# A mixture of experts as a software pipeline: the second layer of a tile behind the first layer of the next, with the weights loaded in that order

## The chip, the core and the metric

The kernel runs on one core of one Trainium2 chip. The metric is the device time of one execution in microseconds; lower is better. The core has TensorE (PE, matmuls; PEld is its weight load), VectorE (DVE), ScalarE (ACT), GpSimd (POOL) and SyncE (SP, which here only issues loads and stores), and 16 DMA engines that all queues share.

## The reference, cut to what matters

One transformer-like layer: an adaptive norm, a time-mixing branch and a recurrent branch, their merge, and then a layer of experts, of which each token takes two out of 32. The change touches only the experts:

```python
for e in range(N_EXPERTS):                      # 32
    he = jax.nn.silu(t @ w1e[e]) * (t @ w3e[e]) # t: 1024 tokens x 1024; w1e, w3e: 1024 x 256
    out = out + cw[:, e:e + 1] * (he @ w2e[e])  # w2e: 256 x 1024; cw is 0 for experts not taken
```

All is in float32.

## The kernel before, in words

Everything before the experts (up to about 1131 us of 1528) and the final norm behind them are the same before and after.

**Lists.** After the router each expert has a list of its tokens. The experts other than 0, 1 and 2 are sorted by load, and the list of each gets a place with a fixed capacity (256, 224, 192, 128, 112, 96, 80, 64 or 32 rows). A *job* is one tile of up to 128 rows. There are 26 jobs: 20 tiles of *single* experts (16 experts; four of them have two tiles), 4 *pairs* (two experts of 64 rows side by side) and 2 *fours* (four experts of 32 rows). The order of the jobs is three singles, a pair, five tiles of singles, a four, a pair, seven tiles of singles, a pair, three tiles of singles, a four, two singles, a pair. What doesn't fit goes to overflow tiles behind all that, in a chain of conditions, of which none runs here.

**Weights.** Each expert is 6 *pieces* of 128 x 1024 float32, 512 KB each: pieces 0 to 3 are the first layer (w1 and w3), pieces 4 and 5 the second (w2). `issue` puts the loads on SP's queue in the order of the list `pieces`; a piece goes to one of `NRAW` = 16 raw buffers (`w`). For a single expert `split` turns a piece into a high part `wh` (cast on ACT to the fast matmul format) and a low part `wl` (raw minus high, on DVE, or on POOL for pieces 4 and 5, except for the first two experts); `NW` = 8 buffers of each. The raw buffer is free again after the split. Pairs and fours use the raw pieces directly, in full float32, and hold them until their matmuls have read them.

**One job.** `gather` fetches the token rows from HBM by an indirect DMA on POOL into one of two buffers `xg`. `turn` transposes them on TensorE (8 transposes) and splits them into `th` and `tl`. `up` is the first layer: 24 matmuls (8 slices of 128 rows, three products high-high, high-low, low-high). `hidden` does SiLU on ACT, the product on DVE (`he`) and two transposes. `down` splits that into `eh` and `el`, runs the second layer, 12 matmuls, multiplies by a row (`yt`, DVE) and scatters the rows by an indirect DMA on POOL. `turn2`, `up2`, `down2` are the same for pairs and fours, without splits, with matmuls on parts of the columns that run side by side.

**Order.** The Python text gives each instruction its priority; a scheduler of the framework puts each engine's instructions into a fixed order at build time, by that priority and by when it believes operands and buffers to be ready. At run time every engine goes through its queue in order. The text of the loop before is, for job n: gather of n+1, first layer of n, transposes of n+1, hidden step and second layer of n, `issue` up to 18 pieces past the job's own, splits of the next expert.

Of the kernel before, what the change touches and what calls it, by code (L numbers as in the profile page):

```python
# [9 lines left out]
F32 = mybir.dt.float32  # L10
# [7 lines left out]
DRAM = bass.MemoryType.DRAM  # L18

NRAW = 16  # L20
NW = 8
LA = 3
ONPOOL = (4, 5)
C0 = math.exp(-0.5)
# [68 lines left out]
def _build(tc, A, out, dump, stop, top):  # L93
# [857 lines left out]
              [tuple(NS + 2 * NP + 4 * i + q for q in range(4)) for i in range(NQ)]]  # L951

    jobs = [((e,), e, 128) for e in range(NF)]
    order, pieces, upto = [], [(e, c) for e in range(NF) for c in range(6)], {e: 6 * e + 6 for e in range(NF)}
    for _, u in sorted(((i + 0.5) / len(us), u) for us in units for i, u in enumerate(us)):
        es = tuple(NF + len(order) + q for q in range(len(u)))
        order += u
        pieces += [(e, c) for c in range(6) for e in es]
        for e in es:
            upto[e] = len(pieces)  # L960
        if len(u) == 1:
            jobs += [(es, t, m) for t, m in tiles_of(u[0])]
        elif len(u) == 2:
            jobs.append((es, NTP + (u[0] - NS) // 2, 128))
        else:
            jobs.append((es, NTQ + (u[0] - NS - 2 * NP) // 4, 128))
    raws, src = {}, {}
    issued = [0]

# [4 lines left out]
    def load(src, c, raw=None):  # L974
        raw = wo.tile([128, 1024], F32, name="w", bufs=NRAW) if raw is None else raw
        Y.dma_start(raw, src[:, c * 1024:c * 1024 + 1024])
        return raw

    def issue(n):

        while issued[0] < min(n, 192):
            e, c = pieces[issued[0]]
            if e not in src:
                src[e] = A["we"][e] if e < NF else chosen(order[e - NF])
            raws[e, c] = load(src[e], c)
            issued[0] += 1
# [332 lines left out]
    with pool("psume", 1, PSUM) as psum, pool("ew", 1) as ew, pool("ex", 2) as ex:  # L1319
# [1 line left out]
        for t in xgb:  # L1321
            P.memset(t, 0.0)

        def split(raw, pool_engine):
            h = ew.tile([128, 1024], F32R, name="wh", bufs=NW)
            l = ew.tile([128, 1024], F32R, name="wl", bufs=NW)
            S.copy(h, raw)  # L1327
            (P if pool_engine else V).tensor_sub(l, raw, h.bitcast(F32))  # L1328
            return h, l

        def gather(n, ti, m):

            xg = xgb[n % 2]
            P.indirect_dma_start(out=xg[0:m], out_offset=None, in_=h2d,
                                 in_offset=bass.IndirectOffsetOnAxis(ap=gidx[0:m, ti:ti + 1], axis=0),
                                 bounds_check=1023, oob_is_err=False)
            return xg

        def turn(xg, m):

            R = slice(0, m)
            th = ex.tile([128, 8, 128], F32R, name="th")
            tl = ex.tile([128, 8, 128], F32R, name="tl")
            for i in range(2):
                pt = psum.tile([128, 4, 128], F32, name="pt", bufs=3)
                for k in range(4):
                    T.transpose(pt[:, k, R], xg[R, (4 * i + k) * 128:(4 * i + k) * 128 + 128], ident[R, R])
                sl = slice(4 * i, 4 * i + 4)
                S.copy(th[:, sl, R], pt[:, :, R])  # L1349
                V.tensor_sub(tl[:, sl, R], pt[:, :, R], th[:, sl, R].bitcast(F32))  # L1350
            return th, tl
# [13 lines left out]
        def hidden(ph, m):  # L1365

            R = slice(0, m)
            he = ex.tile([128, 256], F32, name="he")
            S.activation(he[R], ph[R, 0:256], AF.Silu)
            V.tensor_mul(he[R], he[R], ph[R, 256:512])  # L1370
            pt = psum.tile([128, 4, 128], F32, name="pt", bufs=3)
            for k in range(2):
                T.transpose(pt[:, k, R], he[R, k * 128:k * 128 + 128], ident[R, R])
            return pt
# [3 lines left out]
            P.indirect_dma_start(out=yd, out_offset=bass.IndirectOffsetOnAxis(ap=sidx[R, ti:ti + 1], axis=0),  # L1378
                                 in_=yt[R], in_offset=None, bounds_check=2047, oob_is_err=False)

        def down(W, ph, ti, m):
            R = slice(0, m)
            pt = hidden(ph, m)
            eh = ex.tile([128, 2, 128], F32R, name="eh")
            el = ex.tile([128, 2, 128], F32R, name="el")
            S.copy(eh[:, :, R], pt[:, 0:2, R])
            V.tensor_sub(el[:, :, R], pt[:, 0:2, R], eh[:, :, R].bitcast(F32))
            yt = ex.tile([128, 1024], F32, name="yt")
            for hf in range(2):
                sl = slice(hf * 512, hf * 512 + 512)  # L1390
                py_ = psum.tile([128, 512], F32, name="py", bufs=3)
                for k in range(2):
                    h, l = W[4 + k]
                    o = hf * 512
                    T.matmul(py_[R], eh[:, k, R], h[:, o:o + 512], start=(k == 0), stop=False)
                    T.matmul(py_[R], eh[:, k, R], l[:, o:o + 512], start=False, stop=False)
                    T.matmul(py_[R], el[:, k, R], h[:, o:o + 512], start=False, stop=(k == 1))
                V.tensor_mul(yt[R, sl], py_[R], mrow["gt2"][R, sl])
            scatter(yt, ti, m)
# [3 lines left out]
        def turn2(xg):  # L1403
            tp = ex.tile([128, 8, 128], F32, name="th")
            for i in range(2):
                pt = psum.tile([128, 4, 128], F32, name="pt", bufs=3)
                for k in range(4):
                    T.transpose(pt[:, k], xg[:, (4 * i + k) * 128:(4 * i + k) * 128 + 128], ident)
                S.copy(tp[:, 4 * i:4 * i + 4], pt)
            return tp  # L1410
# [5 lines left out]
        def up2(W, tp):  # L1416
            ph = psum.tile([128, 512], F32, name="ph", bufs=2)
            for k in range(8):
                o = (k % 2) * 512
                for s_, C in parts(W):  # L1420
                    T.matmul(ph[C], tp[:, k, C], W[s_][k // 2][:, o:o + 512], start=(k == 0), stop=(k == 7))  # L1421
            return ph

        def down2(W, ph, ti):
            pt = hidden(ph, 128)
            ep = ex.tile([128, 2, 128], F32, name="eh")
            S.copy(ep, pt[:, 0:2])
            yt = ex.tile([128, 1024], F32, name="yt")
            for hf in range(2):
                sl = slice(hf * 512, hf * 512 + 512)  # L1430
                py_ = psum.tile([128, 512], F32, name="py", bufs=3)
                for k in range(2):
                    for s_, C in parts(W):
                        T.matmul(py_[C], ep[:, k, C], W[s_][4 + k][:, sl], start=(k == 0), stop=(k == 1))
                V.tensor_mul(yt[:, sl], py_, mrow["gt2"][:, sl])  # L1435
            scatter(yt, ti, 128)

        W = {}

        def begin(es):  # L1440
            for e in es:
                if e not in W:
                    W[e] = [raws.pop((e, c)) for c in range(6)]
                    if len(es) == 1:
                        if e < 2:
                            with tc.issue_after(last.ins):
                                W[e] = [split(r, False) for r in W[e]]
                        else:
                            W[e] = [split(r, c in ONPOOL) for c, r in enumerate(W[e])]

        def turned_of(n, xg):
            es, _, m = jobs[n]
            return turn2(xg) if len(es) > 1 else turn(xg, m)

        issue(6 * LA)
        begin(jobs[0][0])
        tt = {0: turned_of(0, gather(0, *jobs[0][1:]))}
        for n, (es, ti, m) in enumerate(jobs):
            nxt = jobs[n + 1] if n + 1 < len(jobs) else None
            if nxt:  # L1460
                xg = gather(n + 1, *nxt[1:])
            pair = len(es) > 1
            ph = up2([W[e] for e in es], tt.pop(n)) if pair else up(W[es[0]], tt.pop(n), m)
            if nxt:
                tt[n + 1] = turned_of(n + 1, xg)
            if pair:
                down2([W[e] for e in es], ph, ti)
            else:
                down(W[es[0]], ph, ti, m)
            if nxt and nxt[0] != es:  # L1470
                issue(max(upto[es[-1]] + 6 * LA, upto[nxt[0][-1]]))
                begin(nxt[0])


        shf, scf, gf = (wo.tile([128, 1024], F32, name="w", bufs=NRAW) for _ in range(3))
# [8 lines left out]
        def nest(o):  # L1484
            if o < NX:
                with tc.If(cnt > o):
                    we = chosen(32 + o)
                    w = [split(load(we, c, ex.tile([128, 1024], F32, name="yt")), c in ONPOOL) for c in range(6)]
                    tt_ = turn(gather(o, NT0 + o, 128), 128)
                    down(w, up(w, tt_, 128), NT0 + o, 128)  # L1490
                    nest(o + 1)
        nest(0)

# [37 lines left out]
```

## Time and profile before

| | |
|---|---|
| median of 3 runs | 1531.28 us (1524.67 to 1535.25) |
| the profiled execution's own time | 1529.99 us |
| its span | 1528.2 us |
| TensorE busy | 1321.9 us, 87% |
| DVE, ACT, POOL busy | 60%, 32%, 26% |
| weight loads of the experts | 192 of 512 KB |
| bytes moved in the whole span | 248.58 MB, mean 163 GB/s |

The span runs from the first to the last instruction; the execution's time is a little longer. Shares over the whole span mix stages with different limits, so the rows below are read by stretches, in us from the span's start. "Waited for" rows give the idle time of an engine and the instruction that ended it. Matmuls are pipelined, so the duration of one (about 0.4 us) is longer than the distance to the next.

### The profile page before, as it was taken

Reading aid. Unit: us, or ns where it says so; the run is one execution under the profiler, and the core shown is the slowest. Engines: PE = TensorE matmul, PEld = TensorE weight load, DVE = VectorE, ACT = ScalarE, POOL = GpSimd, SP = SyncE. Lnnn points to the kernel's source line nnn. Section 1 sums busy time; section 2 is a strip of 40 time slices with the busy share of each in tenths; the row PEclk is TensorE's granted clock in tenths of the full one; section 3 lists DMA queues with packets and bytes.
Section 4 is the critical chain, followed back from the end, with each engine's and each line's share of the span. In section 5 each row is a group of like instructions: output and inputs, shape, how many; then the busy total and the mean of one; then the engine's idle time right before and its main releaser. Section 6 shows DMA issues by size and latency. Waiting matters only on the chain.

```text
span 1528.2 us, 23082 instructions
## 1 busy us (share of the span) xinstructions
PE 1321.9 (87%) x8482; PEld 919.1 (60%) x8482; DVE 917.9 (60%) x2071; ACT 487.0 (32%) x892; POOL 402.5 (26%) x331
## 2 busy tenths in 40 slices
PE   0999899899999999999999798899848998989810
PEld 0776676666776667766666476687645644745400
DVE  8936868687758562475532587724686524653457
ACT  3222323132222222222221594312335423532421
POOL 7001222121101210111111325701214522743314
PEclk9998999899999999999999899999959999999965
DMA  6334432323442211112210654442358979978962
GB/s 263 128 120 138 124 113 90 101 94 115 140 151 87 73 59 36 45 47 69 64 49 27 210 191 147 156 159 95 113 192 299 382 275 401 379 275 313 410 275 101
DMA packets 112827, 248.58 MB, mean 163 GB/s; under 512 B 39056, under 2 KB 40384, under 8 KB 111680
## 3 DMA queue, kind: packets, MB, share of 16 engines
q1 hardware_dynamic: 105952, 230.22, 43.4%
q0 software_dynamic: 6752, 16.79, 3.0%
q8 instruction: 69, 1.13, 0.3%
q14 instruction: 54, 0.44, 0.1%
HBM read 217.11 MB, written 37.31 MB: 166 GB/s over the span
## 4 chain that ended last, share of the span: by engine, by line
PE 58%; DVE 19%; DMA 12%; ACT 4%; issue 4%; POOL 3%; SPq 0%; POOLq 0%; DVEq 0%; ACTq 0%
DMA w<-in_we 9%; PE pg L318 6%; PE pg L319 6%; PE pg L320 6%; PE pj L318 3%; PE pj L320 2%; PE pj L319 2%; PE st L603 2%; DVE wa L228 2%; PE st L617 2%; PE pj L1129 2%; PE pj L1128 2%; PE pj L1127 2%; PE ph L1421 2%; PE ph L1360 1%
## 5 line engine op out<-in xcount | busy, mean ns | idle before, releaser
L318 PE MATMUL pg<-hh,wh 128*128 128x512 f32 x376 | 160.2, 426 | 8.1 <-DVE cr L680 5.9
L319 PE MATMUL pg<-hl,wh 128*128 128x512 f32 x376 | 158.2, 421 | 0.0
L320 PE MATMUL pg<-hh,wl 128*128 128x512 f32 x376 | 156.9, 417 | 0.0
L560 POOL TENSOR_TENSOR WV<-VT,m 128x512 f32<-128x512 f32 x32 | 35.6, 1112 | 371.2 <-PE st L603 283.5
L1327 ACT CAST wh<-w 128x1024 fp32r<-128x1024 f32 x96 | 98.4, 1051 | 56.6 <-PE ph L1362 21.0
L1328 DVE TENSOR_TENSOR wl<-w,wh 128x1024 fp32r<-128x1024 f32 x68 | 89.9, 1346 | 17.3 <-ACT wh L1327 14.2
L228 DVE SCALAR_TENSOR_TENSOR wa<-wa,cb 128x1024 f32<-128x1024 f32 x64 | 80.0, 1257 | 28.7 <-DMA wa<-in_wada 28.7
L318 PEld LDWEIGHTS pg<-hh,wh 128*128 128x128 f32 x376 | 73.0, 194 | 33.3 <-issue 12.5
L216 ACT CAST wh<-wr 128x512 fp32r<-128x512 f32 x88 | 54.4, 618 | 100.2 <-PE pj L319 48.4
L217 DVE TENSOR_TENSOR wl<-wr,wh 128x512 fp32r<-128x512 f32 x72 | 55.1, 766 | 50.9 <-ACT wh L216 50.6
L319 PEld LDWEIGHTS pg<-hl,wh 128*128 128x128 f32 x376 | 72.8, 194 | 17.8 <-issue 4.7
L320 PEld LDWEIGHTS pg<-hh,wl 128*128 128x128 f32 x376 | 72.5, 193 | 17.6 <-issue 4.0
L610 DVE SCALAR_TENSOR_TENSOR St<-St,Dc,st 128x64 f32<-128x64 f32 x128 | 35.4, 277 | 77.8 <-PE st L608 77.7
L318 PE MATMUL pj<-hh,wh 128*128 128x512 f32 x192 | 77.5, 404 | 1.1 <-DVE carry L365 1.1
L320 PE MATMUL pj<-hh,wl 128*128 128x512 f32 x192 | 77.0, 401 | 0.0
L319 PE MATMUL pj<-hl,wh 128*128 128x512 f32 x192 | 75.7, 394 | 0.0
L1328 POOL TENSOR_TENSOR wl<-w,wh 128x1024 fp32r<-128x1024 f32 x28 | 68.6, 2455 | 19.0 <-ACT wh L1327 12.5
L1360 PE MATMUL ph<-wh,th 128*128 128x512 f32 (+4 forms) x160 | 64.8, 407 | 6.2 <-ACT th L1349 5.6
L515 DVE TENSOR_TENSOR X<-X,UC 128x60 f32<-128x60 f32 (+24 forms) x248 | 67.0, 270 | 4.2
L1378 POOL DMA_INDIRECT yd<-yt,sidx x26 | 41.7, 1606 | 99.8 <-DVE yt L1435 41.6
L1361 PE MATMUL ph<-wl,th 128*128 128x512 f32 (+4 forms) x160 | 64.2, 401 | 4.0 <-DVE wl L1328 3.9
L1362 PE MATMUL ph<-wh,tl 128*128 128x512 f32 (+4 forms) x160 | 63.7, 399 | 1.7 <-DVE tl L1350 1.7
(512 smaller groups left out, 3136.1 us busy)
## 6 DMA issues: line engine op xcount, KB each, us to landing
w<-in_we SPq DMA_DIRECT2D x192, 512.0 KB
wa<-in_wada SPq DMA_DIRECT2D x64, 512.0 KB
wr<-in_win SPq DMA_DIRECT2D x72, 256.0 KB
gd<-gt SPq DMA_DIRECT2D x32, 256.0 KB
g<-gd SPq DMA_DIRECT2D x32, 256.0 KB
yy<-yd SPq DMA_DIRECT2D x8, 1024.0 KB
xT<-in_xT SPq DMA_DIRECT2D x8, 512.0 KB
Ui<-Ud SPq DMA_DIRECT2D x32, 128.0 KB
```

Of the source, the lines that this page charges most:

```text
L216: S.copy(h[:, :n], raw)
L217: eng.tensor_sub(l[:, :n], raw, h[:, :n].bitcast(F32))
L228: V.scalar_tensor_tensor(wa, wa, 1.0, cb, op0=OP.mult, op1=OP.mult, accum_out=ccol[:, i:i + 1])
L318: T.matmul(ps, wh[:, o:o + 128], hh[k][:, sl], start=(k == 0), stop=False)
L319: T.matmul(ps, wh[:, o:o + 128], hl[k][:, sl], start=False, stop=False)
L320: T.matmul(ps, wl[:, o:o + 128], hh[k][:, sl], start=False, stop=(k == n - 1))
L515: V.tensor_add(X[:, :nj, s + 1:32], X[:, :nj, s + 1:32], t_)
L1327: S.copy(h, raw)
L1328: (P if pool_engine else V).tensor_sub(l, raw, h.bitcast(F32))
L1360: T.matmul(ph[R], th[:, k, R], h[:, o:o + 512], start=(k == 0), stop=False)
L1361: T.matmul(ph[R], th[:, k, R], l[:, o:o + 512], start=False, stop=False)
L1362: T.matmul(ph[R], tl[:, k, R], h[:, o:o + 512], start=False, stop=(k == 7))
```

## The change

The loop over jobs is written as a pipeline. In iteration n the text now has: gather of n+3, first layer of n+1 (with `issue` and the splits of its pieces 0 to 3 in front), the splits of pieces 4 and 5 of n, hidden step of n, transposes of n+2, second layer of n. The list `pieces` follows that: the first-layer pieces of a unit (a single expert, a pair or a four), then the second-layer pieces of the unit before. The 8 buffers for split pieces become two pools: 5 for first-layer pieces (`whu`, `wlu`) and 3 for second-layer pieces (`whd`, `wld`).

```diff
-NW = 8
+NWU, NWD = 5, 3
...
+    pieces, upto = [], {}
+    for i in range(len(units_) + 1):
+        pieces += [(e, c) for c in range(4) for e in units_[i]] if i < len(units_) else []
+        pieces += [(e, c) for c in (4, 5) for e in units_[i - 1]] if i else []
+        if i:
+            upto[units_[i - 1]] = len(pieces)
...
-        def split(raw, pool_engine):
-            h = ew.tile([128, 1024], F32R, name="wh", bufs=NW)
-            l = ew.tile([128, 1024], F32R, name="wl", bufs=NW)
+        def split(raw, c, pool_engine):
+            n, b = ("u", NWU) if c < 4 else ("d", NWD)
+            h = ew.tile([128, 1024], F32R, name="wh" + n, bufs=b)
+            l = ew.tile([128, 1024], F32R, name="wl" + n, bufs=b)
...
+        def first(n):
+
+            if n < len(jobs):
+                es, _, m = jobs[n]
+                issue(upto[es] + 6 * (LA - 2))
+                begin(es, range(4))
+                ph[n] = up2(weights(es), tt.pop(n)) if len(es) > 1 else up(weights(es), tt.pop(n), m)
...
         issue(6 * LA)
-        begin(jobs[0][0])
-        tt = {0: turned_of(0, gather(0, *jobs[0][1:]))}
+        fetch(0)
+        turned_of(0)
+        fetch(1)
+        fetch(2)
+        first(0)
+        turned_of(1)
         for n, (es, ti, m) in enumerate(jobs):
-            nxt = jobs[n + 1] if n + 1 < len(jobs) else None
-            if nxt:
-                xg = gather(n + 1, *nxt[1:])
+            fetch(n + 3)
+            first(n + 1)
+            begin(es, (4, 5))
             pair = len(es) > 1
-            ph = up2([W[e] for e in es], tt.pop(n)) if pair else up(W[es[0]], tt.pop(n), m)
-            if nxt:
-                tt[n + 1] = turned_of(n + 1, xg)
+            pt = hidden(ph.pop(n), 128 if pair else m)
+            turned_of(n + 2)
             if pair:
-                down2([W[e] for e in es], ph, ti)
+                down2(weights(es), pt, ti)
             else:
-                down(W[es[0]], ph, ti, m)
-            if nxt and nxt[0] != es:
-                issue(max(upto[es[-1]] + 6 * LA, upto[nxt[0][-1]]))
-                begin(nxt[0])
+                down(weights(es), pt, ti, m)
```

`fetch(n)` is the gather of job n, `turned_of(n)` its transposes, `begin(es, cs)` takes the raw pieces `cs` of the experts and splits them where the expert is a single one, `weights(es)` hands the pieces to the matmuls. No instruction of the computation is added or removed.

## Rows read from the trace of the kernel before

**Rows 1.** Stretches: PE, PEld, DVE, ACT, POOL busy (count), clock, DMA share, GB/s.
```profile
1131.00:1180.00 49.00, 39.96 (x176) 29.31 (x177) 33.67 (x42) 25.54 (x33) 22.25 (x13) 0.88 0.87 291
1180.00:1216.00 36.00, 34.44 (x163) 22.30 (x160) 19.46 (x27) 17.75 (x27) 18.75 (x11) 1.00 1.02 387
1216.00:1250.00 34.00, 33.12 (x190) 17.92 (x188) 10.52 (x19) 9.65 (x19) 11.63 (x9) 1.00 0.73 247
1250.00:1336.00 86.00, 76.38 (x325) 45.68 (x324) 44.13 (x54) 35.96 (x50) 38.25 (x21) 1.00 1.02 393
1336.00:1366.00 30.00, 26.77 (x119) 15.64 (x118) 15.85 (x18) 13.07 (x19) 16.24 (x9) 0.94 0.69 245
1366.00:1390.00 24.00, 20.84 (x102) 12.62 (x100) 12.17 (x16) 9.08 (x17) 8.20 (x6) 1.00 1.02 394
1390.00:1408.00 18.00, 17.89 (x100) 9.29 (x104) 4.57 (x9) 2.14 (x7) 6.88 (x6) 1.00 0.61 207
1408.00:1450.00 42.00, 37.13 (x176) 18.91 (x170) 18.75 (x23) 17.44 (x24) 14.84 (x8) 1.00 1.02 409
```
**Rows 2.** Waits of SP's queue, expert stage: total us, times, longest.
```profile
SPq L976 <- DVE wl L1328: 54.0, 37, 10.9
SPq L976 <- POOL wl L1328: 40.7, 18, 3.1
```
**Rows 3.** Timeline of TensorE: start, duration, line (first and 21st of a run).
```profile
1210.02 0.39 PE L1360 MATMUL ph<-wh,th 128*128 128x512 f32 x1
...
1214.56 0.39 PE L1362 MATMUL ph<-wh,tl 128*128 128x512 f32 x1
```
**Rows 4.** Waits of TensorE, 1148 to 1236.
```profile
PE ph L1360 <- ACT th L1349: 3.1, 6, 1.1
PE pt L1373 <- DVE he L1370: 2.9, 4, 2.0
```
**Rows 5.** Waits of TensorE, 1291 to 1354.
```profile
PE pt L1373 <- DVE he L1370: 3.9, 3, 3.2
PE ph L1360 <- ACT th L1349: 1.3, 3, 0.6
```
**Rows 6.** Waits of TensorE, 1354 to 1400.
```profile
PE ph L1362 <- DVE tl L1350: 1.7, 1, 1.7
PE ph L1360 <- ACT th L1349: 1.2, 3, 0.5
```
**Rows 7.** The chain that ended last, one piece of it.
```profile
1165.20 5.09 DMA w<-in_we
```
**Rows 8.** Timeline of DVE and TensorE around 1339 (idle time in brackets).
```profile
1334.62 7.62 DVE L1328 TENSOR_TENSOR wl<-w,wh 128x1024 fp32r<-128x1024 f32 x4
...
1342.63 0.41 PE L1373 MATMUL pt<-ident,he 112*128 112x112 f32 x2 [3.18 <-DVE he L1370]
```
**Rows 9.** Groups by line, 1100 to 1530: busy us, mean ns, idle before.
```profile
L1327 ACT CAST wh<-w 128x1024 fp32r<-128x1024 f32 x95 | 97.4, 1052 | 56.6 <-PE ph L1362 21.0 <-DMA w<-in_we 14.3 <-issue 10.7
L1328 DVE TENSOR_TENSOR wl<-w,wh 128x1024 fp32r<-128x1024 f32 x68 | 89.9, 1346 | 17.3 <-ACT wh L1327 14.2 <-DMA w<-in_we 2.6
L1328 POOL TENSOR_TENSOR wl<-w,wh 128x1024 fp32r<-128x1024 f32 x28 | 68.6, 2455 | 19.0 <-ACT wh L1327 12.5 <-issue 6.2
...
L1378 POOL DMA_INDIRECT yd<-yt,sidx x26 | 41.7, 1606 | 99.8 <-DVE yt L1435 41.6 <-DVE yt L1398 32.9 <-DMA w<-in_we 11.7
...
L1334 POOL DMA_INDIRECT xg<-h2d,gidx x26 | 28.4, 1092 | 93.2 <-PE pt L1347 50.7 <-PE pt L1408 22.1 <-DVE ef L1309 18.5
```
**Rows 10.** Line 1328: durations in ns, least, median, most.
```profile
L1328 DVE TENSOR_TENSOR wl<-w,wh x68: 1206/1221/3422, 1126.2 to 1438.4; 128x1024 fp32r<-128x1024 f32 x68
...
L1328 POOL TENSOR_TENSOR wl<-w,wh x28: 2354/2402/3018, 1157.0 to 1442.9; 128x1024 fp32r<-128x1024 f32 x28
```
**Rows 11.** Timeline of the end of the stage.
```profile
1440.52 4.73 POOL L1328 TENSOR_TENSOR wl<-w,wh 128x1024 fp32r<-128x1024 f32 x2
...
1456.23 3.70 PE L1434 MATMUL py<-w,eh 128*64 128x512 f32 x16 [0.46 <-ACT eh L1427]
```

More of the change, by code (lines that the diff above doesn't have):

```diff
@@ L953, in _build @@
     jobs = [((e,), e, 128) for e in range(NF)]
-    order, pieces, upto = [], [(e, c) for e in range(NF) for c in range(6)], {e: 6 * e + 6 for e in range(NF)}
+    order, units_ = [], [(e,) for e in range(NF)]
     for _, u in sorted(((i + 0.5) / len(us), u) for us in units for i, u in enumerate(us)):
@@ L957, in _build @@
         order += u
-        pieces += [(e, c) for c in range(6) for e in es]
-        for e in es:
-            upto[e] = len(pieces)
+        units_.append(es)
         if len(u) == 1:
@@ L1379, in scatter, with down @@
                                  in_=yt[R], in_offset=None, bounds_check=2047, oob_is_err=False)
-        def down(W, ph, ti, m):
+        def down(W, pt, ti, m):
             R = slice(0, m)
-            pt = hidden(ph, m)
             eh = ex.tile([128, 2, 128], F32R, name="eh")
@@ L1422, in up2, with down2 @@
             return ph
-        def down2(W, ph, ti):
-            pt = hidden(ph, 128)
+        def down2(W, pt, ti):
             ep = ex.tile([128, 2, 128], F32, name="eh")
@@ L1438, in _build, with begin @@
         W = {}
-        def begin(es):
+        def begin(es, cs):
             for e in es:
[L1442 to L1449, printed above, removed]
@@ L1451, in turned_of @@
-        def turned_of(n, xg):
-            es, _, m = jobs[n]
-            return turn2(xg) if len(es) > 1 else turn(xg, m)
-        issue(6 * LA)
-        begin(jobs[0][0])
-        tt = {0: turned_of(0, gather(0, *jobs[0][1:]))}
+                for c in cs:
+                    if (e, c) not in W:
+                        W[e, c] = raws.pop((e, c))
+                        if len(es) == 1:
+                            if e < 2:
+                                with tc.issue_after(last.ins):
+                                    W[e, c] = split(W[e, c], c, False)
+                            else:
+                                W[e, c] = split(W[e, c], c, c in ONPOOL)
@@ new lines, in weights, with fetch, turned_of @@
+        def weights(es):
+            w = [{c: W.get((e, c)) for c in range(6)} for e in es]
+            return w if len(es) > 1 else w[0]
+        xg, tt, ph = {}, {}, {}
+        def fetch(n):
+            if n < len(jobs):
+                xg[n] = gather(n, *jobs[n][1:])
+        def turned_of(n):
+            if n < len(jobs):
+                es, _, m = jobs[n]
+                tt[n] = turn2(xg[n]) if len(es) > 1 else turn(xg[n], m)
+        def first(n):
+            if n < len(jobs):
+                es, _, m = jobs[n]
+                issue(upto[es] + 6 * (LA - 2))
+                begin(es, range(4))
+                ph[n] = up2(weights(es), tt.pop(n)) if len(es) > 1 else up(weights(es), tt.pop(n), m)
@@ L1487, in nest @@
                     we = chosen(32 + o)
-                    w = [split(load(we, c, ex.tile([128, 1024], F32, name="yt")), c in ONPOOL) for c in range(6)]
+                    w = [split(load(we, c, ex.tile([128, 1024], F32, name="yt")), c, c in ONPOOL) for c in range(6)]
                     tt_ = turn(gather(o, NT0 + o, 128), 128)
-                    down(w, up(w, tt_, 128), NT0 + o, 128)
+                    down(w, hidden(up(w, tt_, 128), 128), NT0 + o, 128)
                     nest(o + 1)
```

## The prediction

> **What bounds the kernel now.** I read first the table of stretches, because the change touches only the expert stage, from the first gather at 1131 us to the last result at 1461 us. The stage has two masters in turn [rows 1]. In 1180–1216, 1250–1336, 1366–1390 and 1408–1450 the DMA engines are full (share 1.02, up to 409 GB/s); there TensorE is the one that waits. In 1216–1250, 1336–1366 and 1390–1408 the DMA share falls to 0.73, 0.69 and 0.61 while TensorE is busy 33.1 of 34, 26.8 of 30 and 17.9 of 18 us; there TensorE sets the pace. One 512 KB weight piece costs 0.524 MB / 409 GB/s = 1.28 us of a full DMA system.
>
> Second, the waits of the queue that issues the loads [rows 2]: 54.0 and 40.7 us on the two engines that finish a split. A load starts when one of the 16 raw buffers is given back, and for a single expert the split gives it back. So the DMA idles not for want of work but because the lookahead is full.
>
> Third, TensorE's pace and its own waits. From the 1st to the 21st of a run of first-layer matmuls it goes 1210.02 to 1214.56, so 0.227 us each [rows 3]. A single expert's tile is 24 + 12 matmuls, 8.2 us, and with ten transposes some 9.3 us; the tile of that stretch needed 9.6. The waits are short and of one kind: on `he` (DVE) before the transposes of the hidden layer, and on `th` (ACT) before the next tile's first layer [rows 4 to 6]. They are the two places where nothing else is left in TensorE's queue.
>
> **The change part by part.**
>
> *First layer of the next tile ahead of the hidden step.* No instruction is added or removed: the same loads, casts, subtractions, matmuls, gathers and scatters. Behind `first(n+1)`, `hidden(n)` has a whole first layer, 5.4 us, as cover, where its chain (SiLU, multiply) now holds TensorE for up to 3.2 us [rows 5]. `turned_of(n+2)` is finished a tile before its use, so the `th` waits go too. What the three TensorE-bound groups of tiles lose to these waits now:
> - 1148–1236: 3.1 + 2.9 us [rows 4]. The longest, 2.0, stands behind a landing that the chain of waits shows for 1165.20 to 1170.29 [rows 7]; it is a DMA wait in the end, so it is left out: 4.0.
> - 1291–1354: 3.9 + 1.3 = 5.2 us [rows 5]. The big one, 3.18, is DVE's queue: four `wl` subtractions took 7.62 us in front of `he` [rows 8].
> - 1354–1400: 1.7 + 1.2 = 2.9 us [rows 6]. What is in front of the first layer there is `tl`, of the same sort.
>
> Together 12.1 us. In a stretch where the DMA is full, a saved wait can only run into a weight that has not landed. By the share of the three groups that lies outside the full stretches (52 of 88 us, 18 of 63, 22 of 46 [rows 1]), with the 3.2 counted whole because it stands at 1339, where the share is 0.69: 2.4 + 0.6 + 3.2 + 1.4 = 7.6 us. Between 7.6 and 12.1 I take **−10**, the middle: a full DMA system with 16 buffers ahead does not mean that the very next piece is missing, but the chain of waits has landings in it [rows 7]. The DMA's idle time behind each group (34 x 0.27 = 9.2, 30 x 0.31 = 9.3, 18 x 0.39 = 7.0 us [rows 1]) is larger than what each group gives, so the loads can follow.
>
> *Weights loaded as used.* The pieces of a unit are now 4 of its first layer, then the 2 of the unit before. The bytes are the same, and the lookahead of `issue` is 18 pieces ahead of use as before. All 192 loads stay on SP in one queue. Moved past them is nothing but themselves.
>
> *Split pairs in two pools.* 5 + 3 instead of 8. From single to single this is the same room (4 + 1 and 2 + 1 against 6 + 2). At a single expert followed by a pair or a four, the four or pair needs no split buffers. Before, the last two pieces of the single stood split while 16 pieces of the next unit filled the raw buffers; now those two come behind the 16 and wait. That is 2 x 1.28 = 2.6 us less lookahead, at the three places where the DMA idles for fullness: 0 to +7.7. Against it the next single's first layer comes two pieces sooner at the far end of the same stretch. I take **+2**.
>
> *The second layer's splits on POOL.* This is the wait that the change adds. With three buffers the second low part of tile n gets its buffer only when `down(n-1)` lets go of the first of its own, near its end. Then come the cast on ACT (1.05), the subtraction on POOL (2.46, at most 3.02), and on POOL's queue in front of it perhaps the scatter (1.61) and the gather (1.09) [rows 9, 10]: 3.5 to 6.8 us. Cover until its first use: 24 matmuls 5.4, ten transposes 1.2, four matmuls 0.9, so 7.5 us. If it fails, the rest of the second layer, and behind it on TensorE the whole next first layer, stand still. 14 experts split on POOL (28 subtractions [rows 9]); 0 to +24 (worked out under the rivals). It nearly fits: **+2**.
>
> *Gathers three tiles ahead.* Two `xg` buffers still; the buffer of tile n+3 was read when tile n+1 was turned, an iteration before, so POOL no longer stands in a gather waiting for TensorE. Off the path: 0. If that cover went, a gather would cost POOL 1.09.
>
> *The end.* Now the last single's two second-layer subtractions (1440.52, 4.73 us on POOL) hold its second layer, the last pair's first layer comes behind that, and the pair's second layer ends 1456.23 + 3.70 = 1459.9 [rows 11]. Then the order is first layer of the pair, second of the single, second of the pair (3.7). The split that is late then has only 4 pieces behind it, 5.1 us, instead of 12. With the last weight at about 1450, where the full stretch ends [rows 1], it lands near 1445; with 1.05 and two subtractions of 2.4, the first overlapping the landing, it is split near 1449.5; the remaining 1.8 us of that second layer and 3.7 of the pair end near 1455. That is −5; if POOL is kept by a scatter again, +3 (two scatters). I take **−4**.
>
> Sum: −10 + 2 + 2 − 4 = −10. The profiled execution took 1529.99 us, of which the span is 1528.2; it is 1.3 below the median of the runs, 1531.28. So 1520 for that execution, **1521** on the median.
>
> **Where a rule of the chip notes is weighed.** The DMA falls idle in three stretches while all raw buffers are taken [rows 1, 2]. The Trainium skill (Perfetto Trace Analysis, Optimization Strategy) says that the same gap coming back on the engine that ought to be full can mean too few buffers for the next tile. This change adds none, so by the rule the three gaps stay, and the sum would be the end's part alone, near 1527; that is the second rival below, which the rows above carry without it.
> The `wl` subtraction on DVE takes 1.22 at the median, 1.35 in the mean and 3.42 at most [rows 9, 10]: 68 x 0.13 = 8.5 us, some seven subtractions held up by 1.2. The Trainium skill (SBUF — State Buffer, Who interferes with whom) has it that a VectorE instruction with two SBUF inputs and a GpSimd one that reads SBUF shut each other out. If by it all 28 of POOL's held one up, DVE would have 21 x 1.2 = 25 us more work, and the time would go to that of the slower rival.
>
> **The rivals.**
> - *Already pipelined.* The instructions are put in order by a scheduler, and the waits for `th` are only some 0.5 us each (3.1 in 6 [rows 4]), which suggests that other work already stands in them. If the new text gives nearly the old order, only the end gains: about 1527 (1524 to 1531). For it: the small waits. Against: the 3.2 and the 2.0, which the order did not cover. Chance 0.13.
> - *Fullness decides.* The waits go, but TensorE then meets weights that have not landed, since 16 + 8 buffers hold no more than before: 1527 to 1533. For it: full DMA in 188 of 330 us. Against: DMA idle behind every group. Chance 0.15.
> - *Slower: POOL's second-layer split comes late.* If POOL takes the first piece of the tile after next ahead of the one needed, the chain is 1.05 + 3.02 + 1.61 + 1.09 + 2.46 = 9.2 against 7.5: 1.7 on each of 14 experts, +24. With the gains, 1530 − 14 + 24 = 1540, 1541 on the median; with DVE held up as well, to 1550. It decides from 7.5 us on. For it: POOL waits in line today before scatters. Against: POOL is busy only 0.34 to 0.54 of the stretches [rows 1]. Chance 0.2.
> - *Much faster.* All of TensorE's idle time of 1180 to 1450 goes (1.6 + 0.9 + 9.6 + 3.2 + 3.2 + 0.1 + 4.9 = 23.5 [rows 1]) and the end gives 4: 1504. Against: 19.2 of it lies where the DMA is full. Chance 0.1.
> - *The forecast*, 1512 to 1530: 0.42.
>
> **How the numbers follow.** Bounds of the terms: −12 to −7.6, 0 to +7.7, 0 to +24, −5 to +3. The range 1503 to 1546 reaches from the much faster case to the middle of the slower one and leaves out about 2 in 10. One per cent, about what a measurement of this kernel can tell from no change, is 15 us: below 1516 lie the much faster case and nearly half of the forecast's lower side, 0.32; above 1546 the worse part of the slower case, 0.16; the rest 0.52.
>
> **What would show it.** Right: TensorE's waits on `he` and `th` near zero in the groups of singles, tiles at 9.3 to 9.4 us, the DMA's idle stretches shorter by some 3 us each, the last second layer right behind the last landing. Wrong: waits of the second layer's matmuls on POOL's `wl`, a DVE busy beyond today's, or the same DMA-full time with new waits of the first layer on the casts. What I can see least is the order that the scheduler makes of the new text.

## The result, and the profile after

| | before | after |
|---|---|---|
| median | 1528.77 us (1523.19 to 1535.25, 20 runs) | 1521.3 us (1510.33 to 1529.92, 20 runs) |
| ratio to before | 1 | 0.9948, 95% interval 0.9927 to 0.9968 |
| span of the profiled execution | 1528.2 us | 1516.0 us |

The change gains 7.5 us, half a per cent. The work ahead of the stage is the same program, but its end differs by some 5 us between these two executions: the first gather is issued at 1131.05 before and at 1126.44 after. Read from there to the first addition of a result (`x<-yy`, 1472.10 and 1459.90), the stage goes from 341.05 to 333.46 us, 7.6 less, which agrees with the medians. On the clock of the trace the stage ends about 12 us earlier. The stretches after the change, with the columns of [rows 1]; the last one below is TensorE's idle end:

```profile
1180.00:1216.00 36.00, 35.89 (x180) 25.34 (x179) 23.14 (x31) 21.51 (x32) 19.98 (x13) 1.00 1.00 375
1216.00:1250.00 34.00, 31.28 (x179) 15.41 (x180) 7.32 (x15) 6.19 (x13) 10.43 (x8) 1.00 0.83 301
1250.00:1336.00 86.00, 78.59 (x347) 50.31 (x348) 48.58 (x59) 38.95 (x55) 38.75 (x22) 1.00 1.01 391
1336.00:1366.00 30.00, 30.00 (x150) 17.44 (x148) 17.98 (x22) 16.61 (x24) 16.27 (x10) 1.00 0.85 291
...
1390.00:1408.00 18.00, 15.21 (x60) 8.80 (x59) 11.02 (x11) 7.65 (x12) 8.52 (x4) 0.81 1.03 408
1408.00:1450.00 42.00, 31.36 (x133) 13.71 (x130) 16.84 (x17) 10.56 (x15) 14.67 (x8) 1.00 0.70 275
1450.00:1461.00 11.00, 0.00 (x0) 0.00 (x0) 1.10 (x1) 0.00 (x0) 0.37 (x1) 0.61 0.57 212
```

The three stretches in which the DMA engines had idled (0.73, 0.69, 0.61 in [rows 1]) stand at 0.83, 0.85 and 1.03. The stretches are fixed on the clock of the trace while the stage moved, so the share from TensorE's first transpose to its last matmul is the safer reading. It went from 0.90 to 0.92, and two shorter gaps stay (share 0.35 in 1222–1228 and in 1336–1342). Before, then after:

```profile
1137.03:1459.94 322.91, 293.48 (x1364) 172.79 (x1364) 154.77 (x198) 131.39 (x193) 134.60 (x77) 0.99 0.90 336
```

```profile
1133.10:1447.50 314.40, 287.69 (x1364) 173.57 (x1364) 160.33 (x198) 131.15 (x193) 130.60 (x77) 0.98 0.92 344
```

TensorE's own waits over the whole stage (line waited for, total us, times, longest) tell the rest. Before:

```profile
PE pt L1373 <- DVE he L1370: 10.0, 11, 3.2
PE ph L1360 <- ACT th L1349: 5.6, 12, 1.1
...
PE py L1396 <- POOL wl L1328: 0.4, 1, 0.4
```

After:

```profile
PE py L1401 <- POOL wld L1334: 8.1, 7, 1.7
PE ph L1367 <- DVE wlu L1334: 5.9, 4, 2.2
...
PE py L1400 <- ACT eh L1391: 4.0, 2, 2.4
PE py L1402 <- DVE el L1392: 3.9, 3, 1.9
PE ph L1366 <- ACT th L1355: 1.4, 2, 1.1
PE pt L1379 <- DVE he L1376: 0.9, 1, 0.9
```

The waits of [rows 4 to 6] have nearly gone: on `he` 0.9 us (10.0 before), on `th` 1.4 (5.6), on `tl` 0.5 (1.7). New ones have come: on the second layer's low parts from GpSimd 8.1 (0.4 before), on `eh` 4.0, on `el` 3.9. Of the two engines that finish a split, the queue of the loads [rows 2] now waits mostly for GpSimd:

```profile
SPq L981 <- POOL wld L1334: 60.9, 16, 7.1
...
SPq L981 <- DVE wlu L1334: 15.9, 19, 1.7
```

Next the subtraction, in groups by line as in [rows 9], and in the last row with least, median and most as in [rows 10]:

```profile
L1334 DVE TENSOR_TENSOR wlu<-w,whu 128x1024 fp32r<-128x1024 f32 x64 | 93.0, 1473 | 22.0 <-ACT whu L1333 20.6
L1334 POOL TENSOR_TENSOR wld<-w,whd 128x1024 fp32r<-128x1024 f32 x28 | 69.8, 2505 | 39.4 <-ACT whd L1333 31.1 <-PE pt L1379 7.9
L1334 DVE TENSOR_TENSOR wld<-w,whd 128x1024 fp32r<-128x1024 f32 x4 | 4.7, 1213 | 0.0
...
L1334 DVE TENSOR_TENSOR wlu<-w,whu x64: 1208/1226/3424, 1121.6 to 1420.1; 128x1024 fp32r<-128x1024 f32 x64
```

VectorE's 68 subtractions take 97.7 us instead of 89.9 at an unchanged median of 1.22 us: some are held up much longer. The end of the stage (before: [rows 11]) shows how. First the chain that ended last, then the timeline of VectorE and GpSimd at the same place:

```profile
1415.63 7.89 DVE wlu L1334 x3
1423.57 0.47 PE ph L1367
...
1437.75 2.36 POOL wld L1334
1440.15 0.47 PE py L1401
```

```profile
1414.50 9.02 DVE L1334 TENSOR_TENSOR wlu<-w,whu 128x1024 fp32r<-128x1024 f32 x4
...
1416.69 5.74 POOL L1334 TENSOR_TENSOR wld<-w,whd 128x1024 fp32r<-128x1024 f32 x2
```

Four subtractions of 1.22 us take 9.02 while two of GpSimd's run beside them, and TensorE waits three times (2.24, 1.47, 1.70 us) in that first layer.

### The profile page after: what moved, and what is told of

Read it like the earlier page. It is cut to its first block, busy times and chain, and to the rows that moved or that the text cites. A ratio compares the mean times of both kernels' runs of the same rounds, so it can differ in the third digit from the quotient of the medians.

```text
span 1516.0 us, 23067 instructions
## 1 busy us (share of the span) xinstructions
PE 1308.0 (86%) x8482; PEld 912.7 (60%) x8482; DVE 923.6 (61%) x2071; ACT 486.4 (32%) x892; POOL 398.6 (26%) x331
## 4 chain that ended last, share of the span: by engine, by line
PE 57%; DVE 20%; DMA 8%; issue 7%; POOL 4%; ACT 3%; POOLq 0%; SPq 0%; DVEq 0%; ACTq 0%
PE pg L319 5%; PE pg L318 5%; PE pg L320 5%; DMA yd<-yt,sidx 3%; PE pj L318 2%; PE pj L319 2%; PE pj L320 2%; PE st L603 2%; DVE wa L228 2%; DMA w<-in_we 2%; PE st L617 2%; PE pj L1134 2%; PE pj L1133 2%; PE pj L1132 2%; PE ph L1426 1%
## 5 line engine op out<-in xcount | busy, mean ns | idle before, releaser
L1334 DVE TENSOR_TENSOR wlu<-w,whu 128x1024 fp32r<-128x1024 f32 x64 | 93.0, 1473 | 22.0 <-ACT whu L1333 20.6
L320 PEld LDWEIGHTS pg<-hh,wl 128*128 128x128 f32 x376 | 71.9, 191 | 17.3 <-issue 4.0
L1334 POOL TENSOR_TENSOR wld<-w,whd 128x1024 fp32r<-128x1024 f32 x28 | 69.8, 2505 | 39.4 <-ACT whd L1333 31.1
L1333 ACT CAST whu<-w 128x1024 fp32r<-128x1024 f32 x64 | 66.4, 1051 | 34.0 <-PE ph L1368 21.0
L1367 PE MATMUL ph<-wlu,th 128*128 128x512 f32 (+4 forms) x160 | 64.6, 404 | 5.9 <-DVE wlu L1334 5.9
L1366 PE MATMUL ph<-whu,th 128*128 128x512 f32 (+4 forms) x160 | 64.3, 404 | 2.1 <-ACT th L1355 1.4
L513 DVE TENSOR_TENSOR UC<-X,Ui 128x60 f32<-128x60 f32 (+24 forms) x248 | 62.5, 252 | 4.4
L1368 PE MATMUL ph<-whu,tl 128*128 128x512 f32 (+4 forms) x160 | 63.8, 399 | 0.0
```

The source lines that it names most:

```text
L320: T.matmul(ps, wl[:, o:o + 128], hh[k][:, sl], start=False, stop=(k == n - 1))
L513: V.tensor_mul(t_, X[:, :nj, s:s + 1].to_broadcast([128, nj, nt]), Ui[:, s, None, s + 1:32].to_broadcast([128, nj, nt]))
L1366: T.matmul(ph[R], th[:, k, R], h[:, o:o + 512], start=(k == 0), stop=False)
L1367: T.matmul(ph[R], th[:, k, R], l[:, o:o + 512], start=False, stop=False)
L1368: T.matmul(ph[R], tl[:, k, R], h[:, o:o + 512], start=False, stop=(k == 7))
```

## The experiments

Each was timed in five rounds against the kernel before. Gains are given as the ratio and, worked out from it, in us of 1528.7 (0.9948 is −7.9).

**The new loop alone.** New loop; the old load order, 18 pieces ahead; one pool of 8.

```diff
-NWU, NWD = 5, 3
+NW = 8
-    for i in range(len(units_) + 1):
...
+    for u in units_:
+        pieces += [(e, c) for c in range(6) for e in u]
+        upto[u] = len(pieces)
...
-                issue(upto[es] + 6 * (LA - 2))
+                issue(upto[es] + 6 * (LA - 1))
```

> Only the loop's new order; the pieces are loaded expert by expert as before, and split pairs share 8 buffers. Ratio to the kernel before (the change itself measured 0.9948). If the gain is the order on TensorE (no more waits on he and th), it is here in full or more: 0.990 to 0.996, with those two waits under 4 us together and the waits on POOL's second-layer splits smaller than in the changed kernel (8.1 us). If the gain comes from loading in the order of use, 0.999 to 1.003. If it comes from the two pools, the same 0.999 to 1.003.

Measured: 1505.36 us, ratio 0.9851 (0.9821 to 0.9881): −22.8 us (−27.4 to −18.2). That is more than was expected, although the waits on `th` and `he` are 6.0 us and not under 4. The longest waits of TensorE over the stage, then two of its stretches, then the whole stage:

```profile
PE ph L1364 <- DVE wl L1331: 3.4, 3, 1.8
PE ph L1363 <- ACT th L1352: 3.2, 5, 1.1
PE py L1397 <- ACT eh L1388: 2.8, 1, 2.8
PE pt L1376 <- DVE he L1373: 2.8, 3, 0.9
```

```profile
1216.00:1250.00 34.00, 31.30 (x182) 14.17 (x182) 7.93 (x14) 4.69 (x11) 9.73 (x10) 1.00 0.90 328
...
1336.00:1366.00 30.00, 30.00 (x151) 18.14 (x148) 18.66 (x25) 14.24 (x22) 15.61 (x10) 1.00 0.98 361
...
1132.85:1437.62 304.77, 284.64 (x1364) 172.74 (x1364) 149.26 (x198) 131.05 (x193) 123.71 (x77) 0.98 0.95 356
```

The loop is worth three times what the whole change is; the remaining two parts give 15 us of it back. With not one buffer more the DMA's gaps nearly close: the share over the stage is 0.95, 0.90 before.

**The change with one pool of 8.** The two names in `split` go back to one.

```diff
-            n, b = ("u", NWU) if c < 4 else ("d", NWD)
-            h = ew.tile([128, 1024], F32R, name="wh" + n, bufs=b)
+            h = ew.tile([128, 1024], F32R, name="wh", bufs=NW)
```

> The change with the split pairs in one pool of 8. If the third buffer of the second-layer pool is what makes the POOL subtraction late, a shared pool gives it an earlier buffer: 0.990 to 0.994 and waits on that subtraction under 5 us. If the pools do not matter, 0.994 to 0.996. If the two pools are the gain, 0.998 or more.

Measured: 1513.02 us, 0.9891 (0.9862 to 0.992): −16.7. Of the 15 us that the change gives back, one pool wins 9. Not by an earlier buffer for GpSimd's subtraction, as was expected: TensorE still waits 7.7 us for its low parts (8.1 in the change).

**The new loop with two pools and the old load order.** As the first experiment, with the pools of 5 and 3.

```diff
-NW = 8
+NWU, NWD = 5, 3
```

> New loop, old load order, two pools of 5 and 3. If the cost sits in the load order (the second layer's pieces land behind the next tile's four), this stays at the loop-only run, 1503 to 1509. If it sits in the smaller pool of 3 for the second layer and of 5 for the first, it is at the changed kernel or near it, 1515 to 1524, with the waits of TensorE on GpSimd's low parts back at some 8 us.

Measured: 1510.64 us, 0.9873 (0.9843 to 0.9904): −19.4. It lies between the two ranges expected. With the two before it this makes a square: from the loop alone (−22.8) the load order costs 6 and the pools 3, neither of which the intervals tell from none; together they cost 15. With the other already in place the cost is clear of the intervals (load order 11.5, pools 8.7); whether the two make each other worse these runs can't tell. Neither is alone in lengthening VectorE's subtractions. The loop alone, then with the new load order, then with the two pools (beside these 64 four more of 4.7 us):

```profile
L1331 DVE TENSOR_TENSOR wl<-w,wh 128x1024 fp32r<-128x1024 f32 x68 | 85.8, 1285 | 22.0 <-ACT wh L1330 20.7
```

```profile
L1333 DVE TENSOR_TENSOR wl<-w,wh 128x1024 fp32r<-128x1024 f32 x68 | 91.0, 1361 | 20.0 <-ACT wh L1332 19.2
```

```profile
L1332 DVE TENSOR_TENSOR wlu<-w,whu 128x1024 fp32r<-128x1024 f32 x64 | 89.1, 1412 | 30.1 <-ACT whu L1331 28.6
```

So 68 of them take 85.8, 91.0 and 93.8 us, and 97.7 with both. TensorE's waits for GpSimd's low parts, on the other hand, come with the load order alone: 1.5 us with the loop alone, 7.7 with the new load order, none listed with the two pools.

**The old loop with the new load order and pools.**

```diff
+            n, b = ("u", NWU) if c < 4 else ("d", NWD)
+            h = ew.tile([128, 1024], F32R, name="wh" + n, bufs=b)
...
+        pieces += [(e, c) for c in range(4) for e in units_[i]] if i < len(units_) else []
+        pieces += [(e, c) for c in (4, 5) for e in units_[i - 1]] if i else []
```

> The loop as before, but the pieces loaded in the new order and the split pairs in two pools. If the gain is the loop's order, nothing of it is here: 0.999 to 1.006 (worse than 1 because second-layer pieces now land behind the next unit's first layer). If loading in the order of use is the gain: 0.994 to 0.997.

Measured: 1549.24 us, 1.013 (1.0106 to 1.0155): +19.9, worse than the worst expected. A loop that needs both second-layer pieces before the next first layer stands and waits for them:

```profile
PE pt L1379 <- DVE he L1376: 11.4, 6, 3.5
PE py L1402 <- POOL wld L1334: 10.6, 7, 5.4
```

**One second-layer subtraction from GpSimd to VectorE, in three kernels.**

```diff
-ONPOOL = (4, 5)
+ONPOOL = (5,)
```

In the changed kernel:

> The change with one of the two second-layer subtractions of each single expert moved from POOL to DVE. If POOL's pair of subtractions is what eats part of the gain, TensorE's waits on them fall from 8.1 to under 4 us and SP's from 60.9 to under 40, ratio 0.990 to 0.994. If DVE is the tighter engine (its subtractions already take 1.47 us in the mean against 1.23 at the median), the waits move to the first-layer subtractions: 0.996 to 1.002.

Measured: 1506.88 us, 0.9845 (0.982 to 0.9869), 15.7 better than the change. TensorE's waits for GpSimd fall from 8.1 to 4.1 us, the load queue's from 60.9 to 22.6. In the kernel before:

> Kernel before with one edit: of a single expert's two second-layer subtractions one goes from GpSimd to VectorE. If the gain of the same edit in the changed kernel (1521 to 1507) came from GpSimd being late for the pipeline, it is worth little here, since the old loop has both second-layer pieces split well before use, and VectorE gets 14 more subtractions of 1.2 us, 17 us of work that may lengthen the waits on the multiply's output: 1527 to 1540. If GpSimd's 2.4 us subtraction is simply the dearer place whatever the order (it gives raw buffers back later, so loads start later), the old loop gains too: 1512 to 1520.

Measured: 1522.32 us, 0.9952 (0.9928 to 0.9977): −7.3, between the two expectations; the second subtraction on GpSimd costs in the old loop too, but half as much. In the new loop with the old load order and one pool:

> New loop with the old load order, one pool of 8, and one second-layer subtraction moved from GpSimd to VectorE. Theory that the order gives about -23 us and the late second-layer split takes back 15: with the old load order the split is not late, so moving a subtraction adds nothing: 1503 to 1509, with TensorE's waits on GpSimd's low part below 2 us as in the loop-only run. Rival, that GpSimd holds raw buffers in either load order (38.5 us of the load queue's waits in the loop-only run): both gains add up, 1490 to 1499.

Measured: 1505.13 us, 0.9849 (0.9819 to 0.9879), the loop alone again. So what the load order and the pools cost together is bound to GpSimd's second subtraction: without it nothing is left to win by undoing both. In the relieved changed kernel the place near the end shows four subtractions at full speed; GpSimd's began only near their end (1413.11):

```profile
1409.54 4.62 DVE L1334 TENSOR_TENSOR wlu<-w,whu 128x1024 fp32r<-128x1024 f32 x4
1414.08 3.42 DVE L1334 TENSOR_TENSOR wld<-w,whd 128x1024 fp32r<-128x1024 f32 x1
```

The one that met GpSimd's (3.31 us there) took 3.42.

**The same with one pool of 8.**

```diff
-NWU, NWD = 5, 3
-ONPOOL = (4, 5)
+NW = 8
+ONPOOL = (5,)
```

> Changed kernel with one pool of 8 and one second-layer subtraction on VectorE. The pools cost some 8 us in the changed kernel and 4 with the old load order. If they cost by making GpSimd's late splits later, nothing is left to win once GpSimd is relieved: 1503 to 1509, as with two pools. If a pool of 3 or 5 costs of itself, this is the best of all, 1494 to 1501.

Measured: 1509.07 us, 0.9876 (0.9847 to 0.9905): no gain over the two pools, at the upper edge of the first expectation and far from the second.

**The scatter an iteration later.** In the changed kernel scatters wait 26.5 us for the landing of the scatter before them, in the queue in which GpSimd's subtractions stand (no such wait before).

```diff
-            scatter(yt, ti, m)
+            late.append((yt, ti, m))
...
+            while late:
+                scatter(*late.pop(0))
```

> Changed kernel, each scatter issued one tile later, behind the next tile's second-layer subtractions in GpSimd's queue. Scatters waited 26.5 us for the landing of the scatter before them, in the queue in which the subtractions stand. If that is what makes the subtractions late, TensorE's wait of 8.1 us on GpSimd's low parts falls below 4 and the time comes to 1508 to 1514. If the subtractions are late by their own work and their late landing, the time stays within 1518 to 1524, or is 3 to 5 us worse for a scatter that is later at the end.

Measured: 1521.11 us, 0.9952 (0.9924 to 0.998). This run decides nothing: the scheduler of the program gave GpSimd's queue the same order of gathers, subtractions and scatters as in the changed kernel, and the scatters waited the same 26.2 us. It only repeats the change. Whether those waits delay a subtraction stays open; the loop alone has 18.1 us of them and the kernel with no subtraction on GpSimd (below) 20.9, and these two are among the fastest.

**GpSimd's two subtractions apart.** One of the first layer, one of the second.

```diff
-ONPOOL = (4, 5)
+ONPOOL = (1, 5)
```

> Changed kernel; GpSimd still does two subtractions of each split expert, but the second piece of the first layer and the second piece of the second layer instead of both of the second layer: same work of each engine, only not side by side. Theory that the second layer's low parts come late because two of 2.5 us stand in a row behind late landings: TensorE's wait on GpSimd's low parts falls from 8.1 to some 4 and the time to 1505 to 1512, as with one subtraction fewer. Rival, that it is the amount of GpSimd's work (its share of raw buffers held, VectorE's subtractions stretched by it): 1518 to 1524 as the changed kernel.

Measured: 1522.41 us, 0.9963 (0.9943 to 0.9983): where the rival, the amount of GpSimd's work, put it. TensorE's direct waits for GpSimd fall from 8.1 to 5.9 us, but VectorE's operations come late in their place (`el` 11.9), and this is why:

```profile
L1334 DVE TENSOR_TENSOR wlu<-w,whu 128x1024 fp32r<-128x1024 f32 x50 | 87.7, 1773 | 24.4 <-ACT whu L1333 21.7 <-DMA w<-in_we 2.0
L1334 DVE TENSOR_TENSOR wld<-w,whd 128x1024 fp32r<-128x1024 f32 x18 | 28.5, 1598 | 15.2 <-ACT whd L1333 15.2
```

68 subtractions took 116.2 us.

**None on GpSimd.**

```diff
-ONPOOL = (4, 5)
+ONPOOL = ()
```

> Changed kernel with no subtraction on GpSimd: 28 more of 1.2 us on VectorE. If lateness of GpSimd was all that the new load order cost, this stands where one subtraction on GpSimd stood or a little better, 1500 to 1508. If VectorE becomes the bound (some 115 us of subtractions where 33 are moved to it, with the hidden layer's multiply queued among them), the waits on its outputs take the gain back: 1512 to 1525.

Measured: 1502.99 us, 0.985 (0.9819 to 0.9881), with the loop alone and the relieved change the best there is. By groups, and by least, median and most:

```profile
L1334 DVE TENSOR_TENSOR wlu<-w,whu 128x1024 fp32r<-128x1024 f32 x64 | 77.2, 1221 | 11.6 <-ACT whu L1333 10.6
L1334 DVE TENSOR_TENSOR wld<-w,whd 128x1024 fp32r<-128x1024 f32 x32 | 38.5, 1217 | 15.8 <-ACT whd L1333 15.6
...
L1334 DVE TENSOR_TENSOR wld<-w,whd x32: 1208/1216/1226, 1130.4 to 1424.0; 128x1024 fp32r<-128x1024 f32 x32
...
L1334 DVE TENSOR_TENSOR wlu<-w,whu x64: 1207/1224/1228, 1121.3 to 1405.3; 128x1024 fp32r<-128x1024 f32 x64
```

All 96 take 115.7 us, none over 1.228: as long as 68 took with 28 on GpSimd in the experiment above. There the help was worth nothing. GpSimd still does its gathers and scatters here, and they hold up no subtraction of VectorE.

**GpSimd busy for nobody.** VectorE does all 96; GpSimd does 28 operations whose result nothing in the stage needs.

```diff
-            (P if pool_engine else V).tensor_sub(l, raw, h.bitcast(F32))
+            V.tensor_sub(l, raw, h.bitcast(F32))
+            if pool_engine and c == 4:
+                P.tensor_sub(x1[:, 7], x1[:, 7], h.bitcast(F32))
+                P.tensor_add(x1[:, 7], x1[:, 7], h.bitcast(F32))
```

> VectorE does all 96 subtractions, as in the run with none on GpSimd (1503), and GpSimd does 28 operations of the old form and size whose result nobody waits for: per expert it takes the high part of the second layer's first piece from the last residual tile and adds it again, which alters that tile by rounding alone. Theory that GpSimd's subtraction costs because its result and its raw buffer come late: nothing waits for it here, so 1500 to 1507 and VectorE's subtractions at 1.22 in the mean. Theory that it costs by holding up VectorE's subtractions (1.44 in the mean in the changed kernel, 1.71 with the split over both layers, 1.22 with GpSimd idle): the mean rises to 1.4 or more, 17 us or more of VectorE's time, and the time to 1511 to 1525.

Measured: 1532.46 us, 1.0019 (1.0 to 1.0039), 26 us over the run with GpSimd's subtractions gone, and beyond what either theory gave.

```profile
L1334 DVE TENSOR_TENSOR wlu<-w,whu 128x1024 fp32r<-128x1024 f32 x64 | 98.5, 1563 | 7.8 <-ACT whu L1333 7.0
L1334 DVE TENSOR_TENSOR wld<-w,whd 128x1024 fp32r<-128x1024 f32 x32 | 57.9, 1824 | 15.8 <-ACT whd L1333 15.6
L1336 POOL TENSOR_TENSOR x<-x,whd 128x1024 f32<-128x1024 f32 x14 | 41.6, 2972 | 31.2 <-ACT whd L1333 30.8 <-issue 0.3
```

```profile
1297.17 4.56 DVE L1334 TENSOR_TENSOR wld<-w,whd 128x1024 fp32r<-128x1024 f32 x2
1297.27 3.37 POOL L1336 TENSOR_TENSOR x<-x,whd 128x1024 f32<-128x1024 f32 x1 [1.68 <-ACT whd L1333]
1300.73 3.24 POOL L1337 TENSOR_TENSOR x<-x,whd 128x1024 f32<-128x1024 f32 x1
...
1301.98 3.07 DVE L1334 TENSOR_TENSOR wlu<-w,whu 128x1024 fp32r<-128x1024 f32 x1
```

VectorE's subtractions grow from 115.7 to 156.4 us (+40.7), and GpSimd's own take 2.97 instead of some 2.46. No low part and no raw buffer hangs on GpSimd here. One cast stood 9.5 us for a high-part buffer that GpSimd still read; else nothing in the stage waited for it, and TensorE's waits are on VectorE (`el` 9.5, `tl` 6.7, `wld` 5.3, `wlu` 4.9 us). So late results of GpSimd are not the cause of these 26 us; what is left is that two engines doing such operations at once hold each other up.

Part of the price comes through TensorE's clock. The run with no subtraction on GpSimd is granted the full clock from 1180 to its last matmul; here the clock is below 1.00 in most stretches. At 1340, for example, TensorE stood 3.89 us for `tl`, and from 1344 to 1348 the granted clock is 0.50, the lower of its two levels (1.2 instead of 2.4 GHz). The stretch around it, here and then in that run:

```profile
1336.00:1366.00 30.00, 26.11 (x120) 16.15 (x118) 22.83 (x21) 12.43 (x21) 17.63 (x10) 0.89 0.72 241
```

```profile
1336.00:1366.00 30.00, 30.00 (x150) 19.36 (x146) 16.51 (x24) 10.60 (x18) 7.71 (x7) 1.00 1.02 387
```

In the two profiled executions TensorE's work from first transpose to last matmul takes 329.5 and 298.9 us. Its listed waits in there are 34.6 and 13.4 us, and 56 and 9 of its matmuls start some 0.43 us behind the one before instead of 0.23. An estimate from these rows: 21 us of the 30.6 are waits, 47 x 0.2 = 9 us the lower clock.

## Why the prediction was right, step by step

The forecast, 1521, is the time measured (1521.3), and this is in part luck: two of its terms were mis-sized and nearly cancelled. It also forecast −10 from a median of 1531.28 over 3 runs; measured are −7.5 from 1528.77 over 20.

- **First layer ahead of the hidden step, −10.** The mechanism was right: the waits on `he`, `th` and `tl`, 17.3 us over the stage before, are 6.0 with the loop alone and 2.8 in the change. The size was not: the loop alone gave −22.8, about 9 more than this term and the end's −4 together. From TensorE's first transpose to its last matmul the stage shrank by 18.1 us (322.9 to 304.8), its listed waits by 8.9 (29.0 to 20.1). The other half is mostly in the same waits: the list counts a wait only from the modelled end of the matmul before it, about 0.4 us behind its start, and shorter waits stand in no list. All 1364 matmuls of the stage are in both traces, so the time beyond their usual distance (0.23 us behind a matmul of a single expert, 0.11 behind a transpose, the few at the lower clock left out) can be added up. In front of the hidden layer's transposes it falls from 11.9 to 1.6 us, and in front of the singles' first layers from 17.5 to 11.3. In front of their second layers it rises from 3.5 to 7.7, and the matmuls of pairs and fours take 85.8 us instead of 89.5. These four make 16 of the 18.1 us. So the step that was mis-sized is the price of the waits: it started from 12.1 us of listed waits in three groups of tiles, not from all that was lost in them over the stage, and then took a part off for the DMA-full stretches. How much the discount was wrong by itself no run shows.
- **Weights loaded as used, 0, and the second layer's splits on POOL, +2.** With the pools' +2 that is +4; measured together +14.9. This is the mis-sized term that mattered. The sum asked only whether the low part comes late, and that happened as priced: the slower rival's 1.7 us for each of 14 experts is the longest wait seen, but on 7 of them, 8.1 us in all instead of 24. What GpSimd's subtraction does to VectorE's stood beside the sum, in the paragraph on the rule and in the slower rival's 1550, and was put at nothing in it. With the loop alone VectorE's 68 subtractions take 85.8 us, with the change 97.7; the new load order alone (91.0) and the pools alone (93.8) each do a part of that. A likely reason is the timing: with the old load order the pieces of a tile land as four and two, and VectorE has mostly done its four when GpSimd takes its two; in the new order the two of tile n stand beside the four of tile n+1, as at 1414.50 above. For the pools no run shows the reason, and how the 14.9 us divide is open.
- **Split pairs in two pools.** The +2 under their name is lost lookahead. Alone they cost 3 us, which these runs can't tell from none, and 9 with the new load order; with one subtraction fewer on GpSimd they cost nothing.
- **Gathers three tiles ahead, 0.** TensorE waits for no gather but the first (5.1 us, 4.4 before), as said. But GpSimd still stands in gathers waiting for TensorE, 49.3 and 5.2 us (50.7 and 22.1 before [rows 9]).
- **The end, −4.** Not isolated. The order forecast for it came about, and the last chain no longer contains a landing; but it contains the held-up subtractions of 1415.63 and GpSimd's of 1437.75, and the last scatter waited 3.44 us for the landing of the one before it. The sign named for it, the last second layer right behind the last landing, did not show: TensorE's last matmul ends 23.8 us after the last weight load is issued (1423.7), 17.2 before (1442.8). From the last matmul to the first addition it is 12.4 us as before (12.2).
- **The rivals.** Already pipelined: fell, the order of the instructions is the one of the new text and the waits went. Fullness decides: fell, the time came down without a buffer more. The Trainium skill (Perfetto Trace Analysis, Optimization Strategy) says that the recurring gap can mean too few buffers; here it had another cause, for the order alone took the DMA share of the stage from 0.90 to 0.95 and most of the gaps away. Slower: its mechanism is there at a third of its price, with the contention beside it. Much faster (1504): the loop alone comes to it (1505.36), the change doesn't.
- **The contention.** The rule cited, the Trainium skill (SBUF — State Buffer, Who interferes with whom), agrees with the runs: no subtraction of VectorE over 1.228 us with none on GpSimd, up to 3.97 with some there. My estimate beside it, 25 us on top of the 8.5 of the kernel before if every one of GpSimd's 28 held one up, makes 33.5; the last run's 40.7 exceeds it.

How much of the 15 us that the change gives back is contention and how much lateness is not settled: with both subtractions of GpSimd apart the lateness fell and the contention rose at the same time in all. That in the changed kernel both go with GpSimd's work is shown; with the old loading and one pool the same 28 subtractions cost nothing that these runs can tell (1505.36 with them, 1505.13 with half). The lower clock has a small part: by the estimate above some 2 us, for 26 matmuls of the change start 0.43 us apart and 16 with the loop alone.

With no subtraction on GpSimd, TensorE's work from first transpose to last matmul lasts 298.9 us, and only 13.4 of that are listed waits.

## What to carry to other kernels

When a change reorders loads, look not only at whether each result still comes in time but at which instructions of other engines now run side by side. Work handed to GpSimd is not free because GpSimd is idle: price it by what the other engine's instructions measure while it runs, and try the kernel with that work taken back. A list of waits can count too little: add up the distances from start to start as well. A total that comes out as forecast can hide two errors; run the parts alone before believing the reasons.

## What was unexpected in the hardware

- An elementwise subtraction of 128x1024 on GpSimd and one on VectorE, both with two operands in SBUF, hold each other up: VectorE's goes from 1.22 to as much as 3.97 us, GpSimd's from 2.35 to as much as 3.38 (in the change). 28 operations on GpSimd whose results nothing needed cost VectorE 40.7 us and the kernel 26, some of it through a lower TensorE clock.
- Sharing the subtractions 68 to 28 gave VectorE no relief in one placing: 116.2 us for 68 against 115.7 for 96 with only gathers and scatters on GpSimd.
